# Layer 1's Strassen pairs: two weight sums made by adding transfers, a fourth pair, and the first pair's loads ahead of the stores

## The chip, the cores and the metric

The kernel runs on one core of a Trainium2 chip. A core has TensorE (PE, with its weight loads PEld), VectorE (DVE), ScalarE (ACT), GpSimd (POOL), SyncE (SP, which mostly starts transfers) and 16 transfer (DMA) engines that serve all queues. The metric is the device time of one execution in microseconds, lower is better; the figure given is the median of several runs.

## The reference

Two layers work on x (256 tokens, 2048 columns, float32) and on 256 memory tokens. Each layer does

```
h = rmsnorm(x)
proj = h @ w_in[l]                      # split into ten column groups
y_a = short_gated_conv(...) * silu(a_g) #  768 columns, 6 groups of 128
y_d = diff_attention(...) * silu(d_g)   #  768 columns, 6 heads of 128
y_m = memory_attention(...) * silu(m_g) #  512 columns, 4 heads of 128
x = x + concat(y_a, y_d, y_m) @ w_out[l]
```

The change is in the last line, the product of y (256 x 2048) with w_out[l] (2048 x 2048), and only in layer 1, but for signs.

## The kernel before

y is kept transposed in the tile yT: 16 slices of 128 rows (slices 0 to 5 conv, 6 to 11 differential heads, 12 to 15 memory heads) by 256 tokens. Every float32 operand is held as two float32r parts, hi and lo, and a product is three matmuls: hi*hi, hi*lo, lo*hi. A weight chunk (two slices of 128 rows by 512 columns, 512 KB) is loaded by SP into one of 4 raw tiles (line 291), cast to hi by ScalarE (line 294) and subtracted to lo by VectorE (line 295); there are 4 hi and 4 lo tiles (PARTS, `parts_tiles`, line 283). A chunk is 12 matmuls (2 slices x 2 token tiles x 3, line 305).

The 2048 output columns are four blocks of 512. Blocks 0 and 1 are done first, over the head slices (line 1222) and then over the conv slices (line 1245). Then come block 2 (`near`) and block 3 (`far`) over the slices in `rest`. For some pairs of slices (`paired`) both blocks are done at once by `seven` (line 368): the 2 x 2 product of two token tiles and two slices with two slices and two column blocks takes 7 products instead of 8 (a Strassen scheme with common sums). With a (the first slice's 1024 columns, B11 and B12) and b (the second slice's, B21 and B22), a pair needs B11, B21, B22 and four weight sums, written over a and b by four VectorE subtractions (line 380), and four sums of token tiles. These are made ahead of it by `token_sums` (line 353), driven by `all_sums` (line 1203): one 128 x 512 sum, four of 128 x 128, a cast and a subtraction. The products are written in the order B11 (to x1), B21 (to near, token tile 0), B22 (to far, token tile 0), first sums (x5), second (x7), B21 and B22's sums (near, token tile 1; x6). x1, x5, x6, x7 are four accumulators in PSUM that collect over all pairs; `collect` (line 1256) adds them to the results at the end.

In layer 1 there are three pairs, on slices 6-7, 8-9 and 10-11, placed before chunks 1, 3 and 4 (counted from 0) of the five chunks of block 2 (`places`, line 1249: positions in the list of slices). Tiles a and b of a pair come from the tags sh, e and sh of a pool with two buffers each. Block 3 follows with its five chunks, the last ones arranged so that the very end is short.

When a block is complete, `leave` calls `finish` (line 1225): VectorE adds the accumulators into xs (line 1230), and in layer 1 SP and ScalarE start the stores (line 1235). The four accumulators of blocks 0 and 1 are the ones that near and far use next: near needs block 0's sums done, far needs block 1's. In the kernel before, block 1's `leave` is called inside the first pair, after the four weight sums and ahead of the last two splits (`meanwhile`).

Each engine works its instructions in order. The order is that of a planner that simulates the program; instructions marked `pin` (`keep_in_program_order`) keep the order in which the program issues them. Small jobs that run beside the blocks (generators such as `all_sums` and `collect`) take one step after each chunk (`run_side`, line 231) or when their count of chunks is reached (`later`, line 214).

Of the kernel before, what the change touches and what calls it, by code (L numbers as in the profile page):

```python
# [10 lines left out]
F32 = mybir.dt.float32  # L11
# [3 lines left out]
ALU = mybir.AluOpType  # L15
# [3 lines left out]
P = 128  # L19
D_MODEL = 2048  # L20
SEQ = 256
DEPTH = 2
NT = SEQ // P
# [4 lines left out]
CG = W_CONV // P  # L28
DH = W_DIFF // P
HALF = 64  # L30
MH = W_MEM // P
EPS = 1e-6
NB = 512
# [15 lines left out]
def encoder(ctx: ExitStack, tc: tile.TileContext, x, mem, norm_g, w_in, conv_w, conv_b,  # L49
            dq_g, dk_g, lq1, lk1, lq2, lk2, head_g, mem_norm_g, w_mem_kv, mq_g, mk_g, w_out, out):  # L50
    nc = tc.nc
    x, mem, out = x[0], mem[0], out[0]
# [8 lines left out]
    keep = pool("keep", 1)  # L61
    tmp = pool("tmp", 2)
# [8 lines left out]
    def nm(s):  # L71
        uid[0] += 1
        return f"{s}_{uid[0]}"
# [136 lines left out]
    side, tasks = deque(), []  # L210
# [3 lines left out]
    def later(g, n):  # L214
        due[id(g)] = chunk[0] + n
        return g
# [131 lines left out]
    def product(left, acc, right, first, last):  # L348

        for i, (a, b) in enumerate(((0, 0), (0, 1), (1, 0))):  # L350
            nc.tensor.matmul(acc, left[a], right[b], start=first and i == 0, stop=last and i == 2)  # L351

    def token_sums(stat, k, home):

        f = tmp.tile([P, 2, SEQ], F32, tag="nat", name=nm("f"), bufs=3)
        pin(nc.vector.tensor_tensor(f, stat[:, 0, k:k + 2, :].bitcast(F32), stat[:, 1, k:k + 2, :].bitcast(F32), ALU.add))
        a11, a21, a12, a22 = f[:, 0, 0:P], f[:, 0, P:SEQ], f[:, 1, 0:P], f[:, 1, P:SEQ]
        s = tmp.tile([P, 4, P], F32, tag="nat", name=nm("sums"), bufs=3)
        yield 1
        pin(nc.vector.tensor_tensor(s[:, 0], a21, a22, ALU.add))  # L360
        pin(nc.vector.tensor_tensor(s[:, 2], a11, a21, ALU.subtract))
        pin(nc.vector.tensor_tensor(s[:, 1], s[:, 0], a11, ALU.subtract))
        pin(nc.vector.tensor_tensor(s[:, 3], a12, s[:, 1], ALU.subtract))
        yield 1
        pin(nc.scalar.copy(home[:, 0], s))
        pin(nc.vector.tensor_tensor(home[:, 1], s, home[:, 0].bitcast(F32), ALU.subtract))

    def seven(stat, k, sums, w, col0, c_near, c_far, x, first, last, homes, meanwhile):


        a, b = (pl.tile([P, 2, NB], F32, tag=tag, name=nm("wide")) for pl, tag in homes)
        for j, raw in enumerate((a, b)):
            pin(nc.sync.dma_start(raw.rearrange("p j c -> p (j c)"), w[(k + j) * P:(k + j + 1) * P, col0:col0 + 2 * NB]))

        def split(src, to=None):
            hi, lo = to or parts_tiles()
            return ((hi, pin(nc.scalar.copy(hi, src))), (lo, pin(nc.vector.tensor_tensor(lo, src, hi.bitcast(F32), ALU.subtract))))  # L377

        def minus(dst, v, u):
            pin(nc.vector.tensor_tensor(dst, v, u, ALU.subtract))  # L380

        def side_of(parts, j):
            return [v[:, j] for v, _ in parts]

        one = keep.tile([P, 2, 1, NB], F32R, tag="mga", name=nm("one"))
        b11 = split(a[:, 0:1], (one[:, 0], one[:, 1]))
        minus(a[:, 0], a[:, 1], a[:, 0])
        minus(a[:, 1], b[:, 1], a[:, 1])
        b2 = split(b)
        minus(b[:, 1], b[:, 1], a[:, 0])  # L390
        minus(b[:, 0], b[:, 0], b[:, 1])
        meanwhile()
        t13 = split(a)
        t42 = split(b)

        def tokens(j, t):
            return [stat[:, part, k + j, t * P:(t + 1) * P] for part in range(2)]

        def summed(i):
            return [sums[:, part, i] for part in range(2)]  # L400

        x1, x5, x6, x7 = x
        product(tokens(0, 0), x1, side_of(b11, 0), first, last)
        product(tokens(1, 0), c_near[0], side_of(b2, 0), False, False)
        product(summed(3), c_far[0], side_of(b2, 1), first, False)
        product(summed(0), x5, side_of(t13, 0), first, last)
        product(summed(2), x7, side_of(t13, 1), first, last)
        product(tokens(1, 1), c_near[1], side_of(t42, 0), False, False)
        product(summed(1), x6, side_of(t42, 1), first, last)

    def row_stats(ss, tag):
# [286 lines left out]
    spare, yTs, gates, summed_heads = {}, {}, {}, set()  # L698
# [131 lines left out]
    pin = tc.keep_in_program_order  # L830
# [48 lines left out]
    class Memory:  # L879
# [66 lines left out]
        def split(self, k, turned):  # L946
            for j, pt in enumerate(turned):
                split_T(memT, k + j, pt, None, pin=True)

    mkT, mv, stm, away = [], [], [], []  # L950
# [17 lines left out]
    first, = rows_T(mem_columns, 0, 1)  # L968
# [67 lines left out]
    s = 1  # L1036
    while s < DEPTH * KT:
        l, k = divmod(s, KT)
# [22 lines left out]
        s = group[-1] + 1  # L1061

    for l in range(DEPTH):
# [5 lines left out]
        yT = T_tile("yT")  # L1069
# [40 lines left out]
        mqT = keep.tile([P, MH, SEQ], F32, tag="mqT", name=nm("mqT"))  # L1110
        mga = sheet(keep, "mga")
        acc = x_block([(C_M, NB)])
# [7 lines left out]
        acc = x_block([(C_M + W_MEM, NB)])  # L1120
        for t in range(NT):
            a = tmp.tile([P, NB], F32, tag="nat", name=nm("a"), bufs=3)
# [10 lines left out]
        bgT = None  # L1133
# [53 lines left out]
        acc = x_block([(C_B, NB)])  # L1187
        scaled(both_rows(bg, 0, 4), acc, HR2)
        acc = x_block([(C_B + NB, 256), (C_G + NB, 256)])
        scaled(both_rows(bg, 4, 6), [a[:, 0:256] for a in acc], HR2)  # L1190
        gate(NB, 256, [a[:, 256:512] for a in acc])
        acc = x_block([(C_G, NB)])
        gate(0, NB, acc)
        tasks.append(later(turn_bg(list(range(CG))), 9))
        acc = x_block([(C_X, NB)])
        ux = sheet(keep, "bgx", CG)
        scaled(both_rows(ux, 0, 4), acc, R2)
        acc = x_block([(C_C, NB)])
        times(both_rows(ux, 0, 4), acc)
        tasks.append(later(conv([0, 1, 2, 3], ux), 6))  # L1200
        sums = []

        def all_sums(l, yT, sums):
            for n, tag in enumerate(("mkT0", "v") if l + 1 < DEPTH else ("mkT0", "mkT1", "v")):
                while tag == "v" and (l, MH // 2 - 1) not in summed_heads:
                    yield 1
                sums.append(keep.tile([P, 2, 4, P], F32R, tag=tag, name=nm("sums")))
                yield from token_sums(yT, CG + 2 * n, sums[n])
                yield 1

        tasks.append(later(all_sums(l, yT, sums), 1))
        acc = x_block([(C_X + NB, 256), (C_C + NB, 256)])
# [7 lines left out]
        heads, convs = list(range(CG, KT)), list(range(CG))  # L1220
# [18 lines left out]
        def leave(b, acc, keep_order=lambda i: i, n=5):  # L1239
            finish(b, acc, keep_order)  # L1240
            if not final:
                tasks.append(later(x_next(xT, l + 1, b), n))

        for b in range(2):
            block(yT, w_out[l], [(b * NB, NB)], convs, acc=accs[b])
            if b == 0:
                leave(b, accs[b])

        places = (2, 6, 8) if final else (2, 6)
        paired = [CG + 2 * n for n in range(len(places))]  # L1250
        homes = [((tmp, tag),) * 2 for tag in ("sh", "e", "sh")] if final else [((tmp, "sh"),) * 2, ((keep, "bgx"), (keep, "ga"))]
        rest = [k for k in heads + convs if not CG <= k < CG + 2 * len(places)]
        near, far = accumulators(), accumulators()
        x = [pl.tile([P, NB], F32, tag=tag, name=nm("x")) for pl, tag in ((ps_s, "s"), (ps_s, "s"), (ps_t, "t"), (ps_t, "t"))]

        def collect(near):

            def at(t, b):
                return xs[:, t, b * NB:(b + 1) * NB]

            def plus(dst, v, u):
                pin(nc.vector.tensor_tensor(dst, v, u, ALU.add))

            x1, x5, x6, x7 = x
            u, v = (tmp.tile([P, NB], F32, tag="nat", name=nm("u"), bufs=3) for _ in range(2))
            pin(nc.scalar.copy(u, x1))
            plus(at(0, 2), u, at(0, 2))
            plus(u, u, x6)
            plus(v, u, x7)
            yield 1  # L1270
            plus(at(1, 2), v, at(1, 2))
            if not final:
                leave(2, near, n=3)
            plus(u, u, x5)
            plus(at(0, 3), u, at(0, 3))
            yield 1
            plus(v, v, x5)
            plus(at(1, 3), v, at(1, 3))
            if final:
                leave(2, near)  # L1280

        def pair_at(n):
            def run(near):
                seven(yT, paired[n], sums[n], w_out[l], 2 * NB, near, far, x, n == 0, n == len(paired) - 1,
                      homes[n], (lambda: leave(1, accs[1], pin, 4)) if n == 0 else lambda: None)
                if n == len(paired) - 1:
                    tasks.append(later(collect(near), 5))
                run_side(1)
            return run

        block(yT, w_out[l], [(2 * NB, NB)], rest, acc=near, opened=(False, False),
              between={c: pair_at(n) for n, c in enumerate(places)})
        acc = block(yT, w_out[l], [(3 * NB, NB)], rest, apart=4 if final else 0, acc=far, opened=(True, False))
        leave(3, acc)
# [31 lines left out]
```

## Time and profile before

| what | value |
|---|---|
| median of 3 runs | 919.48 us (918.6 to 920.81) |
| the profiled execution's own time | 919.16 us |
| its span, first to last instruction | 917.4 us |
| busy in the span: PE, DVE, ACT, POOL | 911.9, 720.1, 515.8, 38.3 us |
| transfers over the span | 215.15 MB, 235 GB/s |
| granted TensorE clock | 1.00 |

In the rows that follow, a group stands as line, engine, operation, tile written <- tiles read, shape, count, then durations. A timeline or chain row begins with its start and its length in us; the square bracket at its end is the idle time of that engine just before it and what ended it. "SPq" and "ACTq" rows are transfers being issued. A windows row gives the stretch, its length, the busy us of each engine with its count of instructions, the clock, the share of the transfer engines that was busy and GB/s. A matmul's listed duration overlaps its neighbours', so its pitch is taken from many in a row.

### The profile page before, as it was taken

The page shows a single profiled execution, that of the slowest core. Times are in us where ns is not written, and L with a number is a line of the kernel's source. Part 1 is how long each engine was busy: PE and PEld are TensorE (multiplying, and loading weights), DVE is VectorE, ACT ScalarE, POOL GpSimd, SP SyncE. Part 2 cuts the span into 40 slices and gives each one's busy share as a digit, 9 for nine tenths or more (in the row PEclk, how much of TensorE's full clock was granted, in tenths as well). Part 3 has the DMA queues.
Part 4 walks back from the last instruction along what each step waited for, and adds up shares of the span by engine and source line. Part 5 has one row for each costly group of instructions (what it writes and reads, how often), then busy time and mean ns, then how long its engine had stood idle before and what let it go on. Part 6 is the DMA issues. An engine that isn't in the chain of part 4 may idle for free.

```text
span 917.4 us, 12407 instructions
## 1 busy us (share of the span) xinstructions
PE 911.9 (99%) x4161; PEld 757.3 (83%) x4161; DVE 720.1 (78%) x1293; ACT 515.8 (56%) x798; POOL 38.3 (4%) x68
## 2 busy tenths in 40 slices
PE   9999999999999999999999999999999999999998
PEld 6888888888888888888888888888888888888887
DVE  5579978857799697677789857878898787588786
ACT  5667645675555556445556544578555565546352
POOL 2435010000000000000000000000000000000000
PEclk9999999999999999999999999999999999999999
DMA  8899878886679998979777867986889998968842
GB/s 288 289 243 248 287 247 229 244 222 197 188 206 238 247 256 235 263 243 241 264 215 228 275 203 213 268 239 178 236 231 221 266 260 227 268 215 234 275 161 92
DMA packets 244560, 215.15 MB, mean 235 GB/s; under 512 B 131976, under 2 KB 171720, under 8 KB 244496
## 3 DMA queue, kind: packets, MB, share of 16 engines
q1 hardware_dynamic: 239520, 208.71, 79.3%
q0 software_dynamic: 3776, 4.59, 2.1%
q10 hardware_dynamic: 1200, 1.07, 0.3%
q8 instruction: 32, 0.52, 0.2%
q14 instruction: 32, 0.26, 0.1%
HBM read 193.30 MB, written 21.00 MB: 234 GB/s over the span
## 4 chain that ended last, share of the span: by engine, by line
PE 99%; DMA 0%; ACT 0%; SPq 0%; DVE 0%; issue 0%; ACTq 0%
PE acc L305 92%; PE x L351 2%; PE po L519 1%; PE acc L351 1%; PE s L627 1%; PE po L749 1%; PE s L626 1%; PE acc L933 1%; PE pt L763 0%; DMA raw<-in_w_mem_kv_dram 0%; PE s L683 0%; PE s L681 0%; PE s L682 0%; PE rest L305 0%; ACT hi L915 0%; SPq L833 0%
## 5 line engine op out<-in xcount | busy, mean ns | idle before, releaser
L305 PE MATMUL acc<-hi,xT 128*128 128x512 f32 x1792 | 558.4, 390 | 0.0
L294 ACT CAST hi<-raw 128x1024 fp32r<-128x1024 f32 x270 | 283.9, 1053 | 277.3 <-PE acc L305 200.0
L295 DVE TENSOR_TENSOR lo<-raw,hi 128x1024 fp32r<-128x1024 f32 x270 | 329.0, 1222 | 126.7 <-ACT hi L294 124.5
L305 PEld LDWEIGHTS acc<-hi,xT 128*128 128x128 f32 x1792 | 336.3, 188 | 69.0
L305 PE MATMUL acc<-lo,xT 128*128 128x512 f32 x896 | 349.2, 390 | 0.0
L305 PEld LDWEIGHTS acc<-lo,xT 128*128 128x128 f32 x896 | 168.2, 188 | 33.6
L305 PE MATMUL acc<-hi,yT 128*128 128x512 f32 (+1 forms) x432 | 134.1, 388 | 0.0
L305 PEld LDWEIGHTS acc<-hi,yT 128*128 128x128 f32 x432 | 81.0, 188 | 16.7
L305 PE MATMUL acc<-lo,yT 128*128 128x512 f32 x216 | 83.7, 388 | 0.0
L305 PE MATMUL acc<-hi,memT 128*128 128x512 f32 x248 | 78.0, 392 | 0.0
L305 PEld LDWEIGHTS acc<-hi,memT 128*128 128x128 f32 x248 | 46.2, 188 | 9.3
L916 DVE SCALAR_TENSOR_TENSOR lo<-raw,cva,hi 128x1024 fp32r<-128x1024 f32 (+1 forms) x34 | 41.0, 1218 | 15.4 <-ACT hi L915 15.1
L305 PE MATMUL acc<-lo,memT 128*128 128x512 f32 x124 | 48.0, 391 | 0.0
L305 PEld LDWEIGHTS acc<-lo,yT 128*128 128x128 f32 x216 | 40.6, 188 | 8.4
L915 ACT ACTIVATE hi<-raw,cva 128x1024 fp32r<-128x1024 f32 (+1 forms) x34 | 36.5, 1101 | 12.4 <-DMA raw<-in_w_mem_kv_dram 12.2
L305 PEld LDWEIGHTS acc<-lo,memT 128*128 128x128 f32 x124 | 23.3, 188 | 5.5 <-DVE lo L916 0.8
L377 ACT CAST hi<-wide 128x1024 fp32r<-128x1024 f32 x15 | 15.6, 1050 | 16.3 <-DVE wide L380 6.9
L637 ACT ACTIVATE e<-e,mx 128x256 f32<-128x256 f32 x48 | 23.8, 500 | 1.4 <-DVE mx L633 1.3
L780 POOL DMA_DIRECT2D xt<-in_x_dram x32 | 21.5, 678 | 19.7 <-DVE rsy L189 13.6
L377 DVE TENSOR_TENSOR lo<-wide,hi 128x1024 fp32r<-128x1024 f32 x15 | 18.1, 1220 | 3.5 <-ACT hi L377 3.3
L264 ACT ACTIVATE xT<-xf,gx 128x256 fp32r<-128x256 f32 x32 | 14.3, 503 | 5.7 <-DVE xf L786 5.0
L631 DVE SCALAR_TENSOR_TENSOR e<-dist,s 128x512 f32<-128x512 f32 x24 | 15.7, 680 | 2.2 <-PE s L627 1.7
(210 smaller groups left out, 765.8 us busy)
## 6 DMA issues: line engine op xcount, KB each, us to landing
raw<-in_w_in_dram SPq DMA_DIRECT2D x192, 512.0 KB, 4.6
raw<-in_w_out_dram SPq DMA_DIRECT2D x54, 512.0 KB, 4.8
raw<-in_w_in_dram SPq DMA_DIRECT2D x64, 256.0 KB, 4.3
raw<-in_w_mem_kv_dram SPq DMA_DIRECT2D x30, 512.0 KB, 6.4
d<-sh SPq DMA_DIRECT2D x88, 128.0 KB, 4.2
sh<-d SPq DMA_DIRECT2D x72, 128.0 KB, 4.1
wide<-in_w_out_dram SPq DMA_DIRECT2D x10, 512.0 KB, 7.0
xs<-in_x_dram SPq DMA_DIRECT2D x4, 512.0 KB, 6.3
```

The lines of the kernel that those rows point to most:

```text
L264: both = (nc.scalar.activation(hi, src, AF.Copy, scale=gain), nc.vector.scalar_tensor_tensor(lo, src, gain, hi.bitcast(F32), ALU.mult, ALU ...
L294: nc.scalar.copy(hi, raw)
L295: nc.vector.tensor_tensor(lo_, raw, hi.bitcast(F32), ALU.subtract)
L305: i = nc.tensor.matmul(acc, left, right, start=start, stop=stop)
L351: nc.tensor.matmul(acc, left[a], right[b], start=first and i == 0, stop=last and i == 2)
L377: return ((hi, pin(nc.scalar.copy(hi, src))), (lo, pin(nc.vector.tensor_tensor(lo, src, hi.bitcast(F32), ALU.subtract))))
L519: nc.tensor.matmul(po[:, t, :], eT[:, i, t, k, :], v[:, k, h * P:(h + 1) * P], start=k == 0, stop=k == NT - 1)
L631: nc.vector.scalar_tensor_tensor(e[:, c], dist, -slopes[h], s[c], ALU.mult, ALU.add)
L637: nc.scalar.activation(e[:, c, i], e[:, c, i], AF.Exp, bias=mx[:, c, i:i + 1], accum_out=sm[:, c, i:i + 1])
L780: tc.keep_in_program_order(nc.gpsimd.dma_start(st[:, n], src[n * B:(n + 1) * B].rearrange("p (b r) -> b p r", b=NA)))
L915: both = (nc.scalar.activation(hi[:, j], raw[:, j], AF.Copy, scale=g), nc.vector.scalar_tensor_tensor(lo[:, j], raw[:, j], g, hi[:, j].bit ...
L916: nc.vector.scalar_tensor_tensor(lo[:, j], raw[:, j], g, hi[:, j].bitcast(F32), ALU.mult, ALU.subtract))
```

## The change

- Layer 1's pairs are four, on slices 6-7, 8-9, 10-11 and 12-13 (the last are memory heads), placed before each of the four chunks of block 2 that are left; blocks 2 and 3 have four plain chunks each instead of five. `all_sums` makes a fourth set of token sums, in the tile tag mv.
- The first pair stands ahead of block 2's first chunk, so its products open the near accumulators (`opens`), and block 1's `leave` is called after its last two splits.
- Loading is a function of its own, `load_pair`. In layer 1 it loads a and b as before, loads B11 once more into a third home (256 KB, SP), and then starts on POOL a transfer that reads the far columns of both slices from w_out and adds them to tile a in place (512 KB). That makes the sums B11 + B12 and B12 + B22, and the two VectorE operations for them are left out in layer 1. The signs of the scheme change so that these are additions; the other two weight sums become additions too, and `token_sums` and `collect` follow.
- Each pair's loads are issued at the start of the pair before; the first pair's between block 0's last chunk and block 0's `leave`. Homes of a and b are the tags sh, e, bgx with ga, and sh; homes of the B11 copies are slots of bgT and mqT.
- In layer 1 `collect` starts after 3 steps instead of 5.

```diff
-        pin(nc.vector.tensor_tensor(s[:, 0], a21, a22, ALU.add))
+        pin(nc.vector.tensor_tensor(s[:, 0], a21, a22, ALU.subtract))
...
-        pin(nc.vector.tensor_tensor(s[:, 3], a12, s[:, 1], ALU.subtract))
+        pin(nc.vector.tensor_tensor(s[:, 3], a12, s[:, 1], ALU.add))
...
+    def load_pair(k, w, col0, homes):
+        a, b = (h[:, 0:2] for h in homes[:2])
         for j, raw in enumerate((a, b)):
             pin(nc.sync.dma_start(raw.rearrange("p j c -> p (j c)"), w[(k + j) * P:(k + j + 1) * P, col0:col0 + 2 * NB]))
+        if len(homes) > 2:
+            pin(nc.sync.dma_start(homes[2][:, 0], w[k * P:(k + 1) * P, col0:col0 + NB]))
+            pin(nc.gpsimd.dma_start(a, w[k * P:(k + 2) * P, col0 + NB:col0 + 2 * NB].rearrange("(j p) c -> p j c", p=P),
+                                    accum_op=ALU.add))
...
-        b11 = split(a[:, 0:1], (one[:, 0], one[:, 1]))
-        minus(a[:, 0], a[:, 1], a[:, 0])
-        minus(a[:, 1], b[:, 1], a[:, 1])
+        b11 = split(homes[2] if len(homes) > 2 else a[:, 0:1], (one[:, 0], one[:, 1]))
+        if len(homes) == 2:
+            plus(a[:, 0], a[:, 0], a[:, 1])
+            plus(a[:, 1], a[:, 1], b[:, 1])
         b2 = split(b)
-        minus(b[:, 1], b[:, 1], a[:, 0])
-        minus(b[:, 0], b[:, 0], b[:, 1])
-        meanwhile()
+        plus(b[:, 1], b[:, 1], a[:, 0])
+        plus(b[:, 0], b[:, 0], b[:, 1])
+        if not opens:
+            meanwhile()
         t13 = split(a)
         t42 = split(b)
+        if opens:
+            meanwhile()
...
-        product(tokens(1, 0), c_near[0], side_of(b2, 0), False, False)
+        product(tokens(1, 0), c_near[0], side_of(b2, 0), opens, False)
...
-            for n, tag in enumerate(("mkT0", "v") if l + 1 < DEPTH else ("mkT0", "mkT1", "v")):
-                while tag == "v" and (l, MH // 2 - 1) not in summed_heads:
+            for n, tag in enumerate(("mkT0", "v") if l + 1 < DEPTH else ("mkT0", "mkT1", "v", "mv")):
+                while tag in ("v", "mv") and (l, MH // 2 - 1) not in summed_heads:
...
+        places = (0, 2, 4, 6) if final else (2, 6)
+        paired = [CG + 2 * n for n in range(len(places))]
+        rest = [k for k in heads + convs if not CG <= k < CG + 2 * len(places)]
+        copies = []
+
+        def homes(n):
+            def home(pl, tag, j=2):
+                return pl.tile([P, j, NB], F32, tag=tag, name=nm("wide"))
+
+            ab = (home(keep, "bgx", 3), home(keep, "ga", 3)) if n == len(paired) - (2 if final else 1) else \
+                [home(tmp, "e" if final and n == 1 else "sh") for _ in range(2)]
+            if not final:
+                return ab
+            if n == 0:
+                copies.extend((home(keep, "bgT", 3), home(keep, "mqT")))
+            return *ab, copies[n // 3][:, n % 3:n % 3 + 1]
+
+        loaded = []
+
+        def load_next():
+            if len(loaded) < len(paired):
+                loaded.append(homes(len(loaded)))
+                load_pair(paired[len(loaded) - 1], w_out[l], 2 * NB, loaded[-1])
...
             if b == 0:
+                if final:
+                    load_next()
                 leave(b, accs[b])
 
-        places = (2, 6, 8) if final else (2, 6)
...
-            plus(u, u, x5)
+            minus(u, x5, u)
...
             def run(near):
-                seven(yT, paired[n], sums[n], w_out[l], 2 * NB, near, far, x, n == 0, n == len(paired) - 1,
-                      homes[n], (lambda: leave(1, accs[1], pin, 4)) if n == 0 else lambda: None)
+                load_next()
+                seven(yT, paired[n], sums[n], near, far, x, n == 0, n == len(paired) - 1,
+                      places[n] == 0, loaded[n], (lambda: leave(1, accs[1], pin, 4)) if n == 0 else lambda: None)
                 if n == len(paired) - 1:
-                    tasks.append(later(collect(near), 5))
+                    tasks.append(later(collect(near), 3 if final else 5))
                 run_side(1)
...
-        block(yT, w_out[l], [(2 * NB, NB)], rest, acc=near, opened=(False, False),
+        block(yT, w_out[l], [(2 * NB, NB)], rest, acc=near, opened=(places[0] == 0,) * NT,
               between={c: pair_at(n) for n, c in enumerate(places)})
```

More of the change, by code (lines that the diff above doesn't have):

```diff
@@ L366, in token_sums, with seven @@
         pin(nc.vector.tensor_tensor(home[:, 1], s, home[:, 0].bitcast(F32), ALU.subtract))
-    def seven(stat, k, sums, w, col0, c_near, c_far, x, first, last, homes, meanwhile):
-        a, b = (pl.tile([P, 2, NB], F32, tag=tag, name=nm("wide")) for pl, tag in homes)
+    def load_pair(k, w, col0, homes):
+        a, b = (h[:, 0:2] for h in homes[:2])
         for j, raw in enumerate((a, b)):
             pin(nc.sync.dma_start(raw.rearrange("p j c -> p (j c)"), w[(k + j) * P:(k + j + 1) * P, col0:col0 + 2 * NB]))
+        if len(homes) > 2:
+            pin(nc.sync.dma_start(homes[2][:, 0], w[k * P:(k + 1) * P, col0:col0 + NB]))
+            pin(nc.gpsimd.dma_start(a, w[k * P:(k + 2) * P, col0 + NB:col0 + 2 * NB].rearrange("(j p) c -> p j c", p=P),
+                                    accum_op=ALU.add))
+    def seven(stat, k, sums, c_near, c_far, x, first, last, opens, homes, meanwhile):
+        a, b = (h[:, 0:2] for h in homes[:2])
         def split(src, to=None):
@@ L377, in split, with plus @@
             return ((hi, pin(nc.scalar.copy(hi, src))), (lo, pin(nc.vector.tensor_tensor(lo, src, hi.bitcast(F32), ALU.subtract))))
-        def minus(dst, v, u):
-            pin(nc.vector.tensor_tensor(dst, v, u, ALU.subtract))
+        def plus(dst, v, u):
+            pin(nc.vector.tensor_tensor(dst, v, u, ALU.add))
         def side_of(parts, j):
@@ L407, in seven @@
         product(summed(2), x7, side_of(t13, 1), first, last)
-        product(tokens(1, 1), c_near[1], side_of(t42, 0), False, False)
+        product(tokens(1, 1), c_near[1], side_of(t42, 0), opens, False)
         product(summed(1), x6, side_of(t42, 1), first, last)
@@ L1246, in encoder @@
             if b == 0:
+                if final:
+                    load_next()
                 leave(b, accs[b])
-        places = (2, 6, 8) if final else (2, 6)
-        paired = [CG + 2 * n for n in range(len(places))]
-        homes = [((tmp, tag),) * 2 for tag in ("sh", "e", "sh")] if final else [((tmp, "sh"),) * 2, ((keep, "bgx"), (keep, "ga"))]
-        rest = [k for k in heads + convs if not CG <= k < CG + 2 * len(places)]
         near, far = accumulators(), accumulators()
@@ L1262, in plus, with minus @@
                 pin(nc.vector.tensor_tensor(dst, v, u, ALU.add))
+            def minus(dst, v, u):
+                pin(nc.vector.tensor_tensor(dst, v, u, ALU.subtract))
             x1, x5, x6, x7 = x
@@ L1273, in collect @@
                 leave(2, near, n=3)
-            plus(u, u, x5)
+            minus(u, x5, u)
             plus(at(0, 3), u, at(0, 3))
             yield 1
-            plus(v, v, x5)
+            minus(v, x5, v)
             plus(at(1, 3), v, at(1, 3))
```

## The prediction

> **What bounds the kernel now.** I read the page first, then who TensorE waited for, then its chain in a calm stretch, then the changed stage by windows.
>
> ```profile
> span 917.4 us, 12407 instructions
> ...
> PE 911.9 (99%) x4161; PEld 757.3 (83%) x4161; DVE 720.1 (78%) x1293; ACT 515.8 (56%) x798; POOL 38.3 (4%) x68
> ...
> PE 99%; DMA 0%; ACT 0%; SPq 0%; DVE 0%; issue 0%; ACTq 0%
> ```
>
> TensorE is busy for all but 5.5 us of the span and carries the chain of waits. Whom it waited for, over the whole run:
>
> ```profile
> PE warm L128 <- DVE zeros L123: 1.2, 1, 1.2
> PE acc L933 <- ACT hi L915: 0.8, 1, 0.8
> ```
>
> Two waits, 2.0 us, both in the start-up. So the time is the number of matmuls by their pitch, plus a head and a tail. The pitch, from the chain of waits between 840 and 860 us, and the end of the run (start, duration, engine, line):
>
> ```profile
> 839.84 20.17 PE acc L305 x89
> ```
> ```profile
> 913.53 0.28 PE L305 MATMUL rest<-hi,yT 128*128 128x256 f32 x1
> 913.84 0.42 DVE L1232 TENSOR_TENSOR xs<-rest,xs 128x256 f32<-128x256 f32 x1 [0.32 <-PE rest L305]
> ```
>
> 20.17 / 89 = 0.2266 us a matmul (the 390 ns of the page's groups overlap). After the last matmul come one VectorE sum, the last stores and the end, unchanged by the diff. The stage that changes, by windows (then PE, PEld, DVE, ACT, POOL busy, clock, transfer share, GB/s):
>
> ```profile
> 845.00:885.00 40.00, 40.00 (x178) 33.09 (x177) 30.85 (x42) 19.15 (x22) 0.00 (x0) 1.00 0.77 256
> 885.00:913.00 28.00, 28.00 (x130) 23.30 (x130) 23.72 (x32) 11.48 (x13) 0.00 (x0) 1.00 0.24 76
> 863.40:871.90 8.50, 8.50 (x40) 7.02 (x39) 7.67 (x14) 2.63 (x3) 0.00 (x0) 1.00 1.01 306
> 871.90:898.00 26.10, 26.10 (x116) 21.48 (x115) 23.41 (x27) 15.86 (x17) 0.00 (x0) 1.00 0.43 142
> ```
>
> The clock is 1.00 and TensorE never pauses, but the others are near full: from 863.4 to 871.9 us VectorE works 7.67 of 8.50 us and the transfer engines are full (1.01, 306 GB/s); from 871.9 on VectorE works 23.41 of 26.10 us. A gain there is worth nothing to TensorE; a delay of more than the present lead becomes a pause.
>
> **The change, part by part.**
>
> *Fourth pair.* Heads 12 and 13 go as 7 products x 3 = 21 matmuls in place of 24 (2 slices x 2 column blocks x 2 token tiles x 3). 3 x 0.2266 = 0.68 us, all on the path. Layer 0 keeps two pairs. The head, the tail and the other matmuls are the same. This is the only term that can shorten the run: **-0.68 us**.
>
> *Its token sums.* One more set on VectorE. The third set of before, and VectorE's idle time right behind it:
>
> ```profile
> 817.36 0.69 DVE L356 TENSOR_TENSOR f<-yT 128x512 f32<-128x512 f32 x1
> ...
> 819.94 0.28 DVE L360 TENSOR_TENSOR sums<-f 128x128 f32<-128x128 f32 x1
> ...
> 822.66 0.68 DVE L366 TENSOR_TENSOR sums<-sums,sums 128x512 fp32r<-128x512 f32 x1
> 824.24 1.23 DVE L295 TENSOR_TENSOR lo<-raw,hi 128x1024 fp32r<-128x1024 f32 x1 [0.89 <-ACT hi L294]
> 826.96 1.23 DVE L295 TENSOR_TENSOR lo<-raw,hi 128x1024 fp32r<-128x1024 f32 x1 [1.50 <-ACT hi L294]
> ```
>
> 0.69 + 4 x 0.28 + 0.68 = 2.5 us (the four small ones differ by 0.01). VectorE idles about 1 us per weight chunk from 824 us on, which covers it; without cover it would take 2.5 us from a lead that is 5.8 us (below). 0.
>
> *Signs.* Add for subtract, same shapes: 0.
>
> *Sums by transfer.* What a pair costs VectorE and ScalarE now:
>
> ```profile
> L377 ACT CAST hi<-wide x15: 1035/1052/1057, 458.9 to 892.6; 128x1024 fp32r<-128x1024 f32 x15
> L377 DVE TENSOR_TENSOR lo<-wide,hi x15: 1217/1218/1226, 460.4 to 893.7; 128x1024 fp32r<-128x1024 f32 x15
> ...
> L380 DVE TENSOR_TENSOR wide<-wide x10: 691/692/693, 459.0 to 891.8; 128x512 f32<-128x512 f32 x10
> ...
> L377 DVE TENSOR_TENSOR one<-wide,one x5: 684/685/693, 458.3 to 887.8; 128x512 fp32r<-128x512 f32 x5
> ```
>
> A pair falls from 0.69 + 3 x 1.22 + 4 x 0.69 = 7.11 to 5.73 us. With the plain chunk that follows each pair (1.22) VectorE needs 6.95 us where TensorE takes (21 + 12) x 0.2266 = 7.48. It keeps pace without a reserve to speak of; the 1.38 us saved are off the path: 0.
>
> In return each pair loads 256 KB more on SP and starts a 512 KB adding transfer on POOL, which waits for tile a to land. Nothing is queued behind it on POOL (0.00 busy in the windows above); on VectorE the second pair of sums, two splits and what follows stand behind it. No row shows an adding transfer. The nearest:
>
> ```profile
> sh<-kd POOLq DMA_DIRECT2D x2, 512.0 KB, 6.1
> ```
> ```profile
> L869 POOL DMA_DIRECT2D sh<-kd x2: 557/565/573, 93.6 to 124.7; - x2
> ```
> ```profile
> raw<-in_w_out_dram SPq DMA_DIRECT2D x8, 512.0 KB, 5.3
> wide<-in_w_out_dram SPq DMA_DIRECT2D x4, 512.0 KB, 7.5
> ```
>
> A POOL-issued 512 KB transfer lands in 6.1 us, its issue taking 0.57. An adding one also reads its destination: 512 KB more at 306 GB/s is 1.7 us. I take 6.1 + 1.7 = 7.8 us, nearest that row; the low end is 6.1, the high end two wide loads one after the other, 2 x 7.5 = 15.0.
>
> *The first pair at once.* It starts where the last chunk of block 1 ends:
>
> ```profile
> 874.75 0.69 PE x L351 x3
> ```
> ```profile
> 863.42 1.41 DVE L1230 TENSOR_TENSOR xs<-acc,xs 128x256 f32<-128x256 f32 x4
> 865.00 1.23 DVE L295 TENSOR_TENSOR lo<-raw,hi 128x1024 fp32r<-128x1024 f32 x1 [0.17 <-ACT hi L294]
> ...
> 871.39 1.44 DVE L1230 TENSOR_TENSOR xs<-acc,xs 128x256 f32<-128x256 f32 x4 [0.53 <-PE acc L305]
> ```
>
> Its first product stands at 874.75 now, one 12-matmul chunk later than it will: 874.75 - 2.72 = 872.03. Its third product writes the accumulator that the block-1 sums (871.39, the first half ready 0.72 later, 872.11) must have read; that is due at 872.03 + 6 x 0.2266 = 873.39, so 1.3 us to spare. But these sums now stand behind the pair's splits. VectorE from 863.42: 1.41 + 0.69 + 1.22 + 2 x 0.69 + 1.22 + 1.22 = 7.14 us, done at 870.6 if unhindered. The last split gets its buffer when the second chunk of block 1 is used up (872.03 - 12 x 0.2266 = 869.31), so it ends at 869.31 + 1.05 + 1.22 = 871.6: the sums slip 0.2 us, inside the 1.3. 0. The adding transfer must land 1.38 + 1.22 + 1.22 + 0.72 = 4.5 us before 873.39: by **868.9**.
>
> *Where its loads stand.* SP's issues of before, and the last readers of the tiles that are reused (sh; bgT for the copy):
>
> ```profile
> 847.67 8.07 SPq L291 DMA_DIRECT2D raw<-in_w_out_dram  x4
> 855.79 0.94 SPq L373 DMA_DIRECT2D wide<-in_w_out_dram  x2
> ...
> 864.02 1.41 SPq L1235 DMA_DIRECT2D out_dram<-xs  x2
> ```
> ```profile
> 790.30 0.68 DVE L729 TENSOR_TENSOR ga<-sh,v 128x512 fp32r<-128x512 f32 x1
> ```
> ```profile
> 850.85 0.42 DVE L1170 TENSOR_TENSOR z<-z,bgT 128x256 f32<-128x256 f32 x1
> ```
>
> The pair's tiles are free since 791 us. Ahead of block 1's loads, a and b go out at 847.7 instead of 855.8, land by 855.2, and the sum by 855.2 + 7.8 = 863.0: 5.9 us early (at 15.0, 1.3 us late). Pair 1's loads stand ahead of the fourth load (about 855): 862.5, then 870.3, due 2.60 us before its fourth product's second matmul at 872.03 + 43 x 0.2266, that is 879.2: in time at either end. Later pairs are due 7.48 us apart; the fourth, whose sh buffers free at 871.6 (above), has its tile a at 879.1 and its sum at 886.9, against 894.2. The stores of block 0 (864.02) are not on the path.
>
> What SP passes: the copy waits for bgT until 851.3, and block 1's loads may stand behind it, 3.6 us late, plus 1 MB of a and b (3.4 us at 306 GB/s), plus the copy (0.9): 0 to 7.9 us. A load of 847.67 lands 5.3 later at 853.0 and is needed at 872.03 - 36 x 0.2266 = 863.87 less a cast and a split, 2.3, that is 861.6. The 8.6 us of room hide it. For the split itself, ScalarE takes it up now at
>
> ```profile
> 855.75 1.06 ACT L294 CAST hi<-raw 128x1024 fp32r<-128x1024 f32 x1 [1.66 <-PE acc L305]
> ```
>
> so it is done by 855.75 + 1.06 + 1.22 = 858.0, the lead of 5.8 us named above. 0.
>
> *Earlier collection.* VectorE is idle before the last sums already, so this frees nothing:
>
> ```profile
> 911.70 0.76 DVE L1230 TENSOR_TENSOR xs<-acc,xs 128x256 f32<-128x256 f32 x2 [2.86 <-PE acc L305]
> ```
>
> **Sum.** The profiled execution took 919.16 us (the span and 1.76 around it): 919.16 - 0.68 = 918.48. It stands 0.32 under the median of the runs, 919.48; against that median **918.8 us**, -0.07%.
>
> **Rivals.**
>
> *A, slower: the adding transfers run one after another and slowly.* From 855.2 in series, the fourth lands at 855.2 + 4T and is due at 879.2 + 2 x 7.48 = 894.2. It is late from T = 9.75 us; the run is slower by over 0.2% (a pause of 2.5 us) from T = 10.4. At T = 12 the pause is 9.0 us: 927.8. For it: it reads two streams, four stand in one queue, 15.0 is not excluded. Against it: the 6.1 us row, and they start at least 7 us apart. 0.20.
>
> *B: block 1's loads starve.* The 7.9 us above and the adding transfer's own 1.7 to 3.4 us fall together on them: 9.6 to 11.3 against 8.6 of room, a pause of 1.0 to 2.7: 919.8 to 921.5. For it: the full transfer engines at 863 to 872; against it: a and b move while SP waits for bgT. 0.12, half of it over the bound.
>
> *C: VectorE keeps POOL from issuing.* If POOL can issue only while VectorE is idle (2.69 of 26.10 us, a tenth), 0.57 becomes 5.5 us; the fourth pair's tile a, whose sh buffer frees at 871.6, lands at 879.1 at the earliest, its sum at 879.1 + 5.5 + 7.8 = 892.4 against 894.2: hidden; with the 15.0 end it is 5.4 late. Middle, 1.8 late: 920.6. No row of before shows POOL issuing against this stage's sums. The Trainium skill, "SBUF — State Buffer", section "Who interferes with whom", speaks against a GpSimd-issued transfer beside VectorE copies, since descriptor writing is locked out, but says that tensor_tensor, the only VectorE operation in this stage's rows, takes just the read side: by that page the sum stays 918.8. 0.04.
>
> *D: a pause under 2 us from the order on VectorE*, such as a 1.22 us chunk split ahead of the block-1 sums: 0.2 + 1.22 against 1.3 of room, and as much again at a later pair: up to 1.1 us, 919.9. 0.11.
>
> *E: faster by over 0.2%.* Would need 1.84 us and three matmuls give 0.68; only the 2.0 us of start-up waits are left, untouched. 0.03.
>
> **How the numbers follow.** 0.2% (1.84 us) is about what a measurement tells from no change. Forecast as reckoned 0.50, A 0.20, B 0.12, C 0.04, D 0.11, E 0.03. Same: 0.50 + 0.11 + 0.04 + 0.06 = 0.71; slower 0.20 + 0.06 = 0.26; faster 0.03. The likeliest case alone spans 917.9 to 919.6 (the three runs shown spread by 2.2). The range, 917.9 to 923.0, takes in B, C, D and a quarter of A, leaving out 0.15 + 0.03.
>
> **What would show it.** Right: three matmuls fewer, no TensorE wait after the start, the adding transfers landing in about 8 us and before VectorE wants them, the first pair directly behind block 1, the tail from last matmul to end unchanged. Wrong: a TensorE wait on a split or on the block-1 sums between 863 and 900 us, VectorE waiting for an adding transfer, or raw loads landing over 8 us late.

## The result, and the profile after

The changed kernel took 923.25 us (median of 6 runs, 922.83 to 924.33) against 919.49 for the kernel before: a ratio of 1.0043, 95% interval 1.003 to 1.0056. It is slower by 3.8 us, where 0.7 less was forecast, and just outside the range (917.9 to 923.0).

The profiled execution of the changed kernel took 923.42 us. Its page, and then whom TensorE waited for:

```profile
span 921.4 us, 12435 instructions
...
PE 911.8 (99%) x4158; PEld 754.9 (82%) x4158; DVE 720.1 (78%) x1297; ACT 516.5 (56%) x801; POOL 43.1 (5%) x72
...
PE 95%; DMA 2%; DVE 1%; ACT 0%; SPq 0%; issue 0%; ACTq 0%
```
```profile
PE acc L351 <- ACT hi L385: 1.3, 1, 1.3
...
PE x L351 <- ACT one L385: 1.0, 1, 1.0
...
PE x L351 <- DVE lo L385: 0.3, 1, 0.3
PE acc L305 <- DVE lo L295: 0.3, 1, 0.3
PE x L351 <- DVE one L385: 0.2, 1, 0.2
```

The three matmuls are gone (4158 against 4161). But the chain of waits is no longer TensorE alone, and there are five new waits in the changed stage: on casts (ACT hi and one, line 385) and splits (DVE lo and one) of the pairs, and on one split of a plain chunk (DVE lo, line 295). (The start-up shows 1.1 us more of waits than before, but the first pair begins on time, so the loss is not there.) Where the five stand, and then the last matmul, from TensorE's timeline (start, length, and in brackets the idle time before):

```profile
874.73 0.50 PE L351 MATMUL x<-lo,sums 128*128 128x512 f32 x1 [0.33 <-DVE lo L385]
...
878.32 0.50 PE L305 MATMUL acc<-lo,yT 128*128 128x512 f32 x1 [0.31 <-DVE lo L295]
...
881.87 0.50 PE L351 MATMUL x<-one,yT 128*128 128x512 f32 x1 [0.96 <-ACT one L385]
882.59 0.73 PE L351 MATMUL x<-one,yT 128*128 128x512 f32 x2 [0.23 <-DVE one L385]
...
886.68 0.50 PE L351 MATMUL acc<-hi,yT 128*128 128x512 f32 x1 [1.26 <-ACT hi L385]
```
```profile
917.78 0.28 PE L305 MATMUL rest<-hi,yT 128*128 128x256 f32 x1
```

The first pair begins at 871.93 us, within 0.1 us of the 872.03 of the working. From there the steps from one matmul's start to the next, where a pause stands between them, are together 4.2 us longer than the pitch of 0.2266 (0.5, 0.5, 1.1, 0.5 and 1.4 at the five rows, 0.1 at a sixth place), and the step behind five of these pauses is another 0.11 us longer. The last matmul starts at 917.78 instead of 913.53: 4.25 us later, which is -0.68 for the three matmuls and 4.9 of delay; the pauses and the steps behind them are 4.7 of it.

What the casts waited for. ScalarE's waits in the stage, then its timeline (ACTq rows are transfers that ScalarE issues):

```profile
ACT hi L385 <- DMA out_dram<-xs: 7.3, 1, 7.3
ACT hi L385 <- DVE wide L388: 6.3, 3, 2.3
ACT one L385 <- PE acc L305: 5.9, 1, 5.9
```
```profile
863.97 1.05 ACT L385 CAST hi<-wide 128x1024 fp32r<-128x1024 f32 x1 [1.14 <-PE acc L305]
867.16 5.03 ACTq L1247 DMA_DIRECT2D out_dram<-xs  x2
872.37 2.00 ACT L385 CAST hi<-wide 128x1024 fp32r<-128x1024 f32 x2 [7.35 <-DMA out_dram<-xs]
874.27 1.04 ACT L294 CAST hi<-raw 128x1024 fp32r<-128x1024 f32 x1
880.25 0.82 ACTq L1247 DMA_DIRECT2D out_dram<-xs  x2
881.20 0.62 ACT L385 CAST one<-wide 128x512 fp32r<-128x512 f32 x1 [5.88 <-PE acc L305]
```

ScalarE casts nothing from 865.0 to 872.4 us. Between its two casts stand the two stores of block 0's second halves (867.16, together 5.03 us: the second is held up inside the row). In the kernel before, block 1's pair of such issues took 1.02 us. The same comes again with block 1's stores: the next cast after 875.3 is at 881.20, right behind the stores at 880.25. What held the second pair shows in the chain that ended last:

```profile
864.72 15.46 DMA raw<-in_w_out_dram
...
880.25 0.34 ACTq L1247
...
881.20 0.04 ACT one L385
```

A load of a weight chunk, issued at 864.72, took 15.46 us to land; then the store went out, then the cast of pair 1. (The list of waits puts this one down to TensorE, which had long been done.) The list of the program's instructions with their waits says why a store should wait for a load (ScalarE's rows):

```
L385 CAST hi<-wide_8075          [waits DMAHW1,DVE,PE]
L1247 DMA out_dram<-xs 128x256   [waits DMAHW1,DVE]
L1247 DMA out_dram<-xs 128x256   [waits DMAHW3,DVE]
L385 CAST hi<-wide_8074          [waits DMASW3,DMAHW0,PE,Activation]
L385 CAST hi<-wide_8075          [waits DVE,PE,Activation]
...
L1247 DMA out_dram<-xs 128x256   [waits DMAHW7,DVE]
L1247 DMA out_dram<-xs 128x256   [waits DMAHW1,DVE]
L385 CAST one<-wide_8076         [waits DMAHW0,PE,Activation]
```

In this program the transfers of SP and ScalarE share eight completion counters (DMAHW0 to 7) in turn, and each waits until the earlier transfer on its counter has landed, eight issues back. Before block 0's stores now stand the loads of pairs 1 and 2 and three chunks. The first store left at 867.16, when a chunk load issued at 855.43 had landed (867.09). The counter of the second store (DMAHW3) was last taken by tile b of pair 2, issued at 856.87 and cast only at 888.0: it landed at 871.78, and the store left at 871.86. In the kernel before, the transfer eight issues ahead of ScalarE's first store had landed at 861.00, 3.2 us before the store was issued. And loads land late now, by the transfers issued from 855 to 857 us:

```profile
wide<-in_w_out_dram SPq DMA_DIRECT2D x2, 512.0 KB, 14.0
raw<-in_w_out_dram SPq DMA_DIRECT2D x1, 512.0 KB, 11.7
```
```profile
845.00:850.00 5.00, 5.00 (x24) 4.14 (x23) 4.38 (x10) 3.51 (x5) 0.00 (x0) 1.00 0.91 313
860.00:865.00 5.00, 5.00 (x24) 4.14 (x23) 3.55 (x6) 2.61 (x3) 1.20 (x1) 1.00 1.07 309
870.00:875.00 5.00, 4.67 (x21) 3.55 (x20) 1.55 (x2) 2.63 (x3) 0.83 (x1) 1.00 1.07 339
```

14.0 us for pair 2's tiles, with the transfer engines full from 845 to 885 us (1.07 from 860 on; 0.77 on average before).

### The profile page after: what moved, and what is told of

It is laid out like the page before. It is cut to its first block, busy times and chain, and to the rows that moved or that the text cites. A ratio compares the mean times of both kernels' runs of the same rounds, so it can differ in the third digit from the quotient of the medians.

```text
span 921.4 us, 12435 instructions
## 1 busy us (share of the span) xinstructions
PE 911.8 (99%) x4158; PEld 754.9 (82%) x4158; DVE 720.1 (78%) x1297; ACT 516.5 (56%) x801; POOL 43.1 (5%) x72
## 3 DMA queue, kind: packets, MB, share of 16 engines
q10 hardware_dynamic: 1200, 1.07, 0.3%
## 4 chain that ended last, share of the span: by engine, by line
PE 95%; DMA 2%; DVE 1%; ACT 0%; SPq 0%; issue 0%; ACTq 0%
PE acc L305 89%; DMA raw<-in_w_out_dram 2%; PE x L351 1%; PE po L531 1%; PE acc L351 1%; DMA raw<-in_w_mem_kv_dram 1%; PE s L639 1%; PE po L761 1%; PE s L638 1%; PE pt L775 0%; ACT hi L385 0%; PE s L695 0%; PE s L693 0%; PE s L694 0%; SPq L908 0%
## 5 line engine op out<-in xcount | busy, mean ns | idle before, releaser
L305 PE MATMUL acc<-hi,yT 128*128 128x512 f32 (+1 forms) x416 | 129.5, 388 | 0.0
L305 PEld LDWEIGHTS acc<-hi,yT 128*128 128x128 f32 x416 | 78.0, 188 | 16.1
L305 PE MATMUL acc<-lo,yT 128*128 128x512 f32 x208 | 80.7, 388 | 0.3 <-DVE lo L295 0.3
L375 POOL DMA_DIRECT2D wide<-in_w_out_dram x4 | 4.8, 1206 | 753.8 <-DMA raw<-in_w_out_dram 728.3
L385 ACT CAST hi<-wide 128x1024 fp32r<-128x1024 f32 x18 | 18.5, 1046 | 17.7 <-DVE wide L388 8.4
L385 DVE TENSOR_TENSOR lo<-wide,hi 128x1024 fp32r<-128x1024 f32 x18 | 21.8, 1221 | 7.6 <-ACT hi L385 7.4
```

The source lines that it names most:

```text
L305: i = nc.tensor.matmul(acc, left, right, start=start, stop=stop)
```

## The experiments

The theory (T): ScalarE's store issues, placed ahead of casts and waiting for late loads of later pairs, delay the casts; VectorE's splits and TensorE follow. Rivals: the loads or adding transfers themselves come too late for the casts (R), or VectorE is too full when pairs stand closer (Q). All ran beside the kernel before, which took 919.1 us each time.

| run | median us | ratio to before, 95% |
|---|---|---|
| stores of blocks 0 and 1 on SP | 918.0 | 0.9988 (0.9979 to 0.9997) |
| the same, again | 918.39 | 0.9993 (0.9984 to 1.0001) |
| these stores on POOL | 918.41 | 0.9995 (0.9987 to 1.0004) |
| put off on ScalarE | 918.07 | 0.9991 (0.9982 to 1.0000) |
| no adding transfers (sums left out) | 918.69 | 0.9997 (0.9988 to 1.0006) |
| four pairs, sums on VectorE | 918.49 | 0.9994 (0.9985 to 1.0003) |
| four pairs, sums on VectorE, stores on SP | 918.34 | 0.9994 (0.9985 to 1.0003) |
| three pairs with adding transfers | 918.7 | 0.9997 (0.9988 to 1.0006) |
| only block 0's stores on SP | 922.22 | 1.0033 (1.0020 to 1.0046) |
| first pair's loads behind block 0's leave | 928.45 | 1.0107 (1.0092 to 1.0123) |
| the kernel before, stores on SP | 919.19 | 1.0000 (0.9991 to 1.0009) |

**Stores on SP.** In `finish`:

```diff
-                        eng = nc.scalar if lo else nc.sync
+                        eng = nc.scalar if lo and b > 1 else nc.sync
```

> The changed kernel, but the second-half stores of blocks 0 and 1 are issued by SP instead of ScalarE. Theory T (ScalarE's store issues wait for an earlier transfer to land, 7.3 us before the first pair's third cast and 5.9 us before pair 1's first cast, and the casts behind them come late): these two waits go, the TensorE waits of 0.3, 0.3, 1.0, 0.2 and 1.3 us between 873 and 887 us go, and the time falls by about 4.5 us to 918.5 to 919.5. Rival R (the traffic of the loads and adding transfers is itself too late for the casts): the time stays at 922 to 924 with the casts waiting for transfers into wide or raw. Rival Q (VectorE is simply full when pairs stand closer): stays at 922 to 924 with VectorE busy without a gap ahead of the pauses.

918.0 us, 5.2 under the changed kernel and half a microsecond below the band. TensorE's waits and ScalarE's timeline:

```profile
PE warm L128 <- DVE zeros L123: 1.2, 1, 1.2
PE acc L945 <- ACT hi L927: 0.4, 1, 0.4
```
```profile
863.44 1.05 ACT L385 CAST hi<-wide 128x1024 fp32r<-128x1024 f32 x1 [1.00 <-PE acc L305]
866.16 1.06 ACT L385 CAST hi<-wide 128x1024 fp32r<-128x1024 f32 x1 [1.67 <-PE acc L305]
868.92 1.05 ACT L385 CAST hi<-wide 128x1024 fp32r<-128x1024 f32 x1 [1.70 <-PE acc L305]
```
```profile
wide<-in_w_out_dram SPq DMA_DIRECT2D x8, 512.0 KB, 10.8
wide<-in_w_out_dram POOLq DMA_DIRECT2D x4, 512.0 KB, 9.0
```

All pauses after the start-up are gone, with the same transfers, as late as before (wide 10.8 us, adding 9.0): R and Q fall. The first pair's three large casts stand 2.7 us apart, each as soon as TensorE frees its buffer.

**Stores on POOL.**

```diff
+                        eng = (nc.scalar if b > 1 else nc.gpsimd) if lo else nc.sync
```

> The same stores on POOL's queue instead of ScalarE's, so that they wait neither in ScalarE nor in SP; pair 1's adding transfer stands behind two stores on POOL. Theory T: 918.5 to 919.5, as with SP. Rival R: 922 to 924. If SP's own order matters (loads behind stores that wait for block sums), this is lower than the SP version by up to 1 us, otherwise equal to it within 0.5 us.

918.41: the same within 0.5 us, no TensorE wait after the start-up. SP's order does not matter here.

**The stores put off, still on ScalarE.** They are collected in `finish` and issued behind the last pair's casts.

```diff
+                        if b < 2 and lo:
+                            put_off.append((to, xc))
...
                 if n == len(paired) - 1:
+                    for to, xc in put_off:
+                        pin(nc.scalar.dma_start(to, xc))
```

> The changed kernel with the four second-half stores of blocks 0 and 1 still issued by ScalarE, but put off until behind the last pair's casts. Same transfers, same adding transfers, same engine. Theory T says it is the place of the stores in ScalarE's order, ahead of casts and behind loads that land late, that costs the 4 us: 918 to 919 here. If issuing stores on ScalarE, or the traffic, is the cause, 921 or more.

918.07. Same engine, same transfers, another place in ScalarE's order: the loss is gone. It is the place.

**Without the adding transfers.** The `gpsimd.dma_start(..., accum_op=ALU.add)` of `load_pair` is taken out.

> The changed kernel without the four adding transfers: tile a is used as loaded, so two of the four weight sums of each pair are left out of the computation. ScalarE still issues its stores. It takes 2 MB of HBM reads and their queue out of the crowded stretch. Theory T with the adding transfers as the chief cause of the crowding: landings get shorter, ScalarE's store waits shrink below 2 us and the time falls to 919 to 920. Theory T with the loads pulled forward as the cause: the waits stay and the time is 922 to 923.5. Rival R in its narrow form (the adding transfer lands too late): 918.5 to 919.

918.69, with two of the four weight sums of each pair missing: ScalarE's stores stay where they are, and the loss goes. Landings of what was issued from 845 to 885 us, in this run, and then in the changed kernel:

```profile
raw<-in_w_out_dram SPq DMA_DIRECT2D x10, 512.0 KB, 6.2
wide<-in_w_out_dram SPq DMA_DIRECT2D x8, 512.0 KB, 7.1
```
```profile
raw<-in_w_out_dram SPq DMA_DIRECT2D x9, 512.0 KB, 7.9
wide<-in_w_out_dram SPq DMA_DIRECT2D x8, 512.0 KB, 8.8
wide<-in_w_out_dram POOLq DMA_DIRECT2D x4, 512.0 KB, 9.6
```

Landings fall from 8.8 to 7.1 us for the pairs' tiles, and the stores are held little: block 0's two take 1.88 us in place of 5.03. So the loss needs both: the traffic that the adding transfers bring, and a store ahead of casts. The time lies in the band of the rival, a late adding transfer, and a little under that of T (919 to 920); the three runs with stores moved, where these transfers are all present, exclude the rival.

**Four pairs, sums on VectorE.** `homes` returns tiles a and b alone, so neither copies nor adding transfers are made.

```diff
-            if not final:
-                return ab
+            return ab
```

> The changed kernel's four pairs and places, with all four weight sums on VectorE as before: no copies of B11, no adding transfers (3.1 MB less). VectorE then needs 8.33 us per pair and chunk where TensorE takes 7.48. By that count alone VectorE falls behind by 0.85 us per pair, against a lead of a few us: a pause of 0 to 2 us. Theory T: the store waits shrink since the transfers are less crowded; 919 to 921. Rival Q: 922 or more.

918.49, half a microsecond below T's band and without a TensorE pause in the stage. VectorE is busy 25.40 of 26.10 us and still not late:

```profile
871.90:898.00 26.10, 26.10 (x116) 21.44 (x115) 25.40 (x31) 15.46 (x17) 0.00 (x0) 1.00 0.38 116
```

**The same with stores on SP**, both edits above:

> Four pairs at the changed kernel's places, all four weight sums on VectorE and all stores of blocks 0 and 1 on SP: neither the adding transfers nor ScalarE's store waits. By theory T and the matmul count, 918.0 to 918.8, equal to the version with adding transfers and stores on SP within 0.5 us; then the adding transfers bring nothing. If VectorE's 1.38 us per pair matter, 0.5 to 2 us more than that version.

918.34, within 0.4 us of the two runs with adding transfers and stores on SP (918.0, 918.39). The adding transfers bring no time that shows here.

**Adding transfers alone**: three pairs at the places of before, `collect` after 5 steps.

```diff
-        places = (0, 2, 4, 6) if final else (2, 6)
+        places = (2, 6, 8) if final else (2, 6)
```

> Adding transfers alone: three pairs at the places of before (ahead of chunks 1, 3 and 4), sums by transfer, ScalarE's stores as in both kernels, no fourth pair. No matmul is saved. T: the stores of blocks 0 and 1 come in the plan ahead of more of the loads, so ScalarE waits less than 2 us: 919 to 920. Rival (the adding transfers themselves make the loss): 922 to 924.

918.7, no TensorE pause in the stage, a little under the expected band. The reason given, ScalarE waiting under 2 us, did not come: its profile has one wait of 7.0 us, up to the first pair's last two casts at 874.91, where the kernel before has one of 5.57 up to 873.29, behind block 1's sums. Of the difference, 1.4 us is the two stores ahead of these casts, which take 2.42 us in place of 1.02. But with a chunk of block 2 ahead of it the first pair is 12 matmuls (2.7 us) later than in the change, and is not kept waiting. So the adding transfers alone do not make the loss. Whether the pairs' earlier places or the fourth pair's traffic must join them, this run, which changes both, does not tell.

**Only block 0's stores on SP.**

```diff
+                        eng = nc.scalar if lo and b != 0 else nc.sync
```

> The changed kernel with only block 0's second-half stores moved from ScalarE to SP; block 1's stay on ScalarE. Theory T says each pair of stores makes its own pauses: block 0's (wait of 7.3 us before the first pair's third cast) the two of 0.3 us at 874 and 878, block 1's (5.9 us before pair 1's first cast) the 1.0, 0.2 and 1.3 us at 881 to 887. Here the first go and the later ones stay: 920.5 to 922. If block 1's wait is only a consequence of block 0's delay, 918 to 919.

922.22, a little above the expected band. The pauses at 874 and 878 us are gone, those behind block 1's stores stay (ScalarE waits 7.2 us), so block 1's wait is not a consequence of block 0's. More was lost than the pauses. Two windows of this run (TensorE's busy time and count first, its granted clock in the third column from the end), then, from the changed kernel's profiled execution, the 3.4 us in which TensorE was busy least after the start-up, and two matmuls of this run:

```profile
877.60:881.00 3.40, 1.68 (x6) 0.87 (x6) 1.02 (x2) 1.92 (x3) 0.00 (x0) 1.00 1.03 374
881.00:884.40 3.40, 3.40 (x9) 2.27 (x8) 3.33 (x4) 1.53 (x2) 1.18 (x1) 0.50 0.89 247
```
```profile
883.30:886.70 3.40, 2.14 (x10) 1.12 (x8) 3.28 (x5) 1.53 (x3) 0.54 (x1) 1.00 0.98 240
```
```profile
882.78 0.63 PE L351 MATMUL acc<-lo,yT 128*128 128x512 f32 x1
883.20 0.63 PE L351 MATMUL acc<-hi,yT 128*128 128x512 f32 x1
```

TensorE was idle for 1.72 of the 3.40 us up to 881.0; then the granted clock was 0.50 for 3.4 us, and seven matmuls came 0.43 us apart instead of 0.23, which cost another 1.4 us. In the changed kernel's profiled execution no such stretch was idle for more than 1.3 us, and the clock stayed at 1.00. The Trainium skill, "TensorE: Matmul & The Clock Gate", section "Part 1: The HAM clock gate (the "warmup" mystery)", puts the fall to half clock behind at least one idle window of about 3.4 us that runs freely. The trace differs in what counts as idle: half of 3.4 us was enough here, and the measurement decides.

**The first pair's loads behind block 0's leave.**

```diff
+                leave(b, accs[b])
                 if final:
                     load_next()
-                leave(b, accs[b])
```

> The changed kernel with the first pair's loads issued behind block 0's leave instead of ahead of it, one part of the change undone. Block 0's stores come ahead of the loads in the plan and wait for older transfers, so ScalarE's first wait goes, by theory T. Block 1's stores still follow the loads of pairs 0 to 2. T: 919 to 921. If the loads' earlier place is what keeps the first pair fed (the rival reading), the first pair comes late and the time is 924 or more.

928.45: T's number was wrong, and the rival reading right. Block 0's stores were not held long (two in 1.46 us), as T had it, but the planner then put the loads of pairs 1 and 2 first and the first pair's at 865 us; ScalarE waited for them:

```profile
ACT one L385 <- DMA wide<-in_w_out_dram: 12.8, 1, 12.8
ACT hi L385 <- DMA wide<-in_w_out_dram: 3.4, 1, 3.4
```
```profile
875.16 1.95 PE L351 MATMUL x<-one,yT 128*128 128x512 f32 x3 [3.63 <-ACT one L385]
...
880.58 0.80 PE L351 MATMUL x<-hi,sums 128*128 128x512 f32 x1 [2.62 <-ACT hi L385]
```

Pauses of 3.6 and 2.6 us, and the granted clock was at 0.50 again, here from 873.5 us, 2.0 us into the first pause, to 883.7:

```profile
870.10:873.50 3.40, 1.43 (x7) 0.85 (x5) 0.00 (x0) 0.00 (x0) 0.19 (x1) 1.00 0.83 330
873.50:876.90 3.40, 1.74 (x3) 1.12 (x4) 1.50 (x2) 1.56 (x2) 3.40 (x3) 0.50 0.27 51
```

Having the loads ahead of the stores is needed for the first pair's early place; what hurts is that the loads of later pairs, too, stand ahead of stores that ScalarE issues.

**Controls.** Stores on SP in the kernel before (the same edit there), and the version with stores on SP once more:

> The kernel before with the second-half stores of blocks 0 and 1 on SP. It has no TensorE pause for them to remove, so by theory T it stays at the time of before within 0.4 us (919.1). If the stores on ScalarE cost something there too, it is lower by 0.5 us or more, and part of the gain of the version with stores on SP is not the fourth pair's.

> The changed kernel with the stores of blocks 0 and 1 on SP, run again beside the two others for its distance from the kernel before: the count of three matmuls gives 0.68 us less than before, and the earlier run gave 1.1 less. Expected 918.0 to 918.6 against about 919.1; a value above 919 would say that the earlier run was lucky.

919.19 against 919.11, no change, so the stores cost nothing before; and 918.39. Four pairs with the stores out of ScalarE's way have medians 0.7 to 1.1 us below the kernel before, about the 0.68 of the three matmuls. But of the five intervals only one lies wholly below 1 (they reach from 0.9979 to 1.0004). So these versions are faster than the changed kernel; that they beat the kernel before is likely by the count, and at the limit of measurement.

## Why the prediction was wrong

- **Matmul count, -0.68 us: right.** 4158 matmuls, and with the pauses removed the medians come out at about that size.
- **"The stores of block 0 (864.02) are not on the path": this is the step that failed.** Every transfer was followed past SP and POOL, but half of these stores are issued by ScalarE (line 1235, `eng = nc.scalar if lo`), in its order, ahead of the first pair's third cast; and the loads moved ahead of them made them wait on landings. The working asked when the stores leave, not what is queued behind them. Block 1's stores did the same to pair 1's first cast. The cost was 4.7 us in pauses and the steps behind them, of 4.9 us of delay. The sign that the prediction named for being wrong, a TensorE wait on a split between 863 and 900 us, came.
- **"7.14 us, done at 870.6 if unhindered" for VectorE, sums slipping by 0.2 us: wrong in the change, for that reason.** The block-1 sums stood at 875.73. With stores on SP the last cast of the first pair starts at 868.92, against the 869.31 of the working, so the count itself was sound.
- **Adding transfers in 7.8 us: undersized.** 9.6 us in the median, and 12.0, 9.9, 9.3 and 7.4 one by one. None was itself what TensorE waited for, as argued. They move their bytes at a higher price than reckoned, see below, and other landings lengthen with them: plain loads, reckoned at 5.3 and 7.5 us, took 7.9 and 8.8 in the median, and those issued at 862.64 and 864.72 took 16.1 and 15.5.
- **Rival B, the crowded transfer engines, had the right pressure and the wrong victim.** The transfer engines were as full as it said, but no TensorE wait fell on block 1's own chunks; what starved was ScalarE, through the completion counters. Its price (1.0 to 2.7 us) was too low, since a held store holds all casts behind it. A, C and D did not occur: POOL's issues took 1.18 to 1.25 us, over the 0.57 reckoned and far from C's 5.5. D's price does not follow from its own terms: 0.2 + 1.22 against 1.3 of room is 0.1 us late, and as much again at a later pair makes 0.2, not 1.1; the range did not rest on it.
- **SP's order, the wait for bgT until 851.3, the token sums, the tail: right.** The copy went out at 851.16, and the runs without pauses end as forecast.
- **Sums by transfer: the saving of 0 was right, a cost of 0 was not.** The VectorE versions show that the 1.38 us saved were never needed. But with ScalarE's stores where the change has them the transfers' traffic was a condition of the loss: 923.25 with it, 918.69 and 918.49 without.

## What to carry to other kernels

When loads are pulled forward, list what every engine issues behind them, stores on a compute engine's queue above all: a store that must wait for an old transfer, as on the shared counters here, stops that engine's arithmetic too. A transfer that costs little in place can cost a lot through the landings that others wait for. Where TensorE carries the chain and is never idle, a change can gain only its matmul count, and should be asked first which cover it spends.

## What the runs showed of the hardware

An adding transfer costs the transfer engines about twice a plain one. The queues of the changed kernel between 845 and 900 us (packets, MB, share of 16 engines; q0 holds only the four adding transfers, q1 SP's transfers):

```profile
q1 hardware_dynamic: 5644, 12.19, 64.1%
q0 software_dynamic: 1088, 2.10, 20.7%
```

q0 takes 20.7% for 2.10 MB, q1 64.1% for 12.19 MB: of the 55 us, 5.4 us per MB against 2.9, 1.9 times as much. Four such transfers filled 11.4 us of all 16 engines. It is not POOL's queue that makes them dear: its plain transfers, between 85 and 130 us of the same execution, took 3.0 us per MB:

```profile
q0 software_dynamic: 793, 2.22, 15.0%
```

The granted clock of TensorE fell to a half behind 3.4 us that held 1.7 us of idleness in two pauses (only block 0's stores on SP) and behind 3.4 us that held 2.0 us (loads behind block 0's leave); it did not behind at most 1.3 us (the changed kernel). Where the line lies between, and how the stretches are laid, these three executions do not tell. In the other executions of the changed kernel it may have fallen: three of the six have a mean granted clock of 0.997, with times like those of the rest.
